# A second level of Strassen in one more product of a feed-forward, with elementwise work moved to GpSimd

## The chip, the cores and the metric

The kernel runs on one core of one Trainium2 chip. The core has five engines with a queue each: TensorE (PE; its weight loads are shown apart as PEld), VectorE (DVE), ScalarE (ACT), GpSimd (POOL) and SyncE (SP), which issues most of the DMA transfers here. TensorE writes to PSUM; the operands of all engines lie in SBUF. The metric is device time in microseconds (us) of one execution, and lower is better. A profiled execution gives, beside its time, a trace of every instruction.

## What is computed

One inference step of a decoder layer over 1040 prompt tokens and 8 sample tokens: a feed-forward, a mixer (two kinds of recurrent heads), a second feed-forward and a final norm. The change is in the two feed-forwards alone:

```
def swiglu(x, wg, wu, wd):
    return (jax.nn.silu(x @ wg) * (x @ wu)) @ wd

h = h + 0.5 * swiglu(rmsnorm(h, n1), w1g, w1u, w1d)
...
h = h + 0.5 * swiglu(rmsnorm(h, n2), w2g, w2u, w2d)
```

All in float32. The model width is 1024, the hidden width 2816.

## The kernel before

**Precision.** Each float32 operand is split into a high part, cast by ScalarE (`hi`, `cast`), and a low part, the rest, subtracted by VectorE (`lo`, `low`). A product of 128x128 weights with a block of tokens is three matmuls (`mm3`, L160): high by high, high by low, low by high.

**Tokens** are in four quarters of Q columns: 262 in the first feed-forward (1048 tokens), 258 in the second (1032). Two quarters make a half, c = 0 or 1.

**Outer level.** For one tile of 128 hidden columns, gate and up are one 2x2 block product by Winograd's form of Strassen's method: rows are gate and up, the inner dimension is the lower and upper 512 of the 1024 inputs, and columns are the two quarters of a half. There are 7 products instead of 8, numbered 1 to 7. `Left` (L443) holds a tile's four weight blocks: 1 and 2 belong to gate, 7 and 4 to up; `load` fetches one, `sum_` forms the blocks 5, 6, 7 and 3. `Blocks` holds the token side. A step of `Unit` (L493) is one product for one half c: 4 blocks of 128 inputs by 3 matmuls, 12 matmuls of Q columns. So a product of one tile has two steps. `post` adds the products up as they come: 1 to z; 6 to v; 5 to x; 7 completes up 1; 4 completes up 0; 2 is accumulated onto 1's PSUM bank and completes gate 0; 3 gives gate 1. Here 0 and 1 are the two quarters of a half. Then gate and up are multiplied by the row factor r of the norm (`times_r`), gate goes through Silu on ScalarE (`silu`), and `product_` multiplies the two to the hidden block.

**Inner level.** Tiles are taken in pairs: 11 pairs per feed-forward (`FP`). In pairs 3 to 10, product 3 of both tiles and of both halves is taken as another 2x2 product (`Inner`, L532): rows are the two tiles, columns the two halves, and the inner dimension is again split in two. Its seven products have 2 blocks by 3 matmuls each, 42 matmuls in place of 4 x 12 = 48. `begin` forms sums and differences of the two weight blocks in place, then four high and low parts; `post` (L633) adds the seven results to both tiles' temporaries. The token operands of this level are made once per feed-forward, in pair 1, by `operands` (L550).

**PSUM.** Outer results lie in pairs of banks, two such pairs at a time (`psum2`); inner ones in four single banks (`psm`).

**Hidden blocks.** `Hidden.jobs` (L936) makes, per pair, the seven token-side blocks of the down projection, again by Strassen: 1, 12, 2 and 3 are the products themselves, and 5, 6, 7 and 4 are four differences that VectorE writes to two further buffers. Seven blocks per pair are stored to DRAM (`hd`), 12 only being used for differences. `down` (L992) loads them by product and group of pairs (`Hidden.load`, L967), splits them and multiplies them with the down weights.

**Order.** In a feed-forward, PE, VectorE, ScalarE and SP execute in the order of the program text; GpSimd's order is not written out. `Steps` (L418) is a list of PE steps; `before(i, fn)` puts work of the other engines ahead of step i. A nested pair has 28 steps: 24 outer, and the inner product's seven in 4. Every work item of a pair has a step number: weights are loaded some 10 steps ahead and cast some 4 ahead of use, and hidden blocks are stored in the steps of the next pair.

**Buffers.** Weights (`r`) have 8 buffers, their split forms (`ws`) 6, temporaries (`t`) 9; of the large slots, `u` has 30 and `s` 8. An engine that is to fill a buffer waits until its last reader is done.

Of the kernel before, what the change touches and what calls it, by code (L numbers as in the profile page):

```python
# [9 lines left out]
F32 = mybir.dt.float32  # L10
# [7 lines left out]
P = 128  # L18
D = 1024
KT = D // P  # L20
NM = 16
# [421 lines left out]
class Left:  # L443
# [12 lines left out]
    def sum_(self, p):  # L456
        x, y, op = {5: (7, 4, ALU.add), 6: (5, 1, ALU.subtract), 7: (1, 7, ALU.subtract), 3: (2, 6, ALU.subtract)}[p]
        if p not in self.raw:
            self.raw[p] = self.K.raw(self.n * P)
        self.K.nc.vector.tensor_tensor(self.raw[p], self.raw[x], self.raw[y], op)  # L460
# [68 lines left out]
ORDER6 = (1, 6, 2, 5, 7, 4), (1, 2, 6, 5, 7, 4)  # L529


class Inner:  # L532
# [4 lines left out]
    def __init__(self, K, ops, op=None):  # L537
        self.K, self.ops = K, ops
        self.op = {} if op is None else op
        self.raw, self.w, self.ps = {}, {}, {}  # L540
        self.then, self.out = {}, {}

    def next(self):
        return Inner(self.K, self.ops, self.op)

    def half(self, c, h):
        n = 2 * self.K.Q
        return tuple(x[:, h * n : h * n + n] for x in self.ops[c].op[3])

    def operands(self):  # L550
# [3 lines left out]
        t = K.slot("u", K.T)  # L554
        a, b, d = t[:, :n], t[:, n : 2 * n], K.slot("s", K.T)[:, :n]
# [23 lines left out]
    def begin(self, S, s0):  # L579

        K, nc = self.K, self.K.nc
        f, g = self.raw.pop(0), self.raw.pop(1)
        tmp = K.slot("u", K.T)
        s = tmp[:, :512]
        self.z, self.v = (tmp[:, 512 + i * K.Q : 512 + i * K.Q + K.Q] for i in range(2))

        def sums():
            nc.vector.tensor_add(s[:, :256], g[:, :256], g[:, 256:])
            nc.vector.tensor_sub(s[:, 256:], s[:, :256], f[:, :256])

        def sum7():
            nc.vector.tensor_sub(g[:, :256], f[:, :256], g[:, :256])

        def sum3():
            nc.vector.tensor_sub(f[:, 256:], f[:, 256:], s[:, 256:])

        def hi(i, src):
            self.w[i] = K.ws()
            nc.scalar.copy(self.w[i][:, : src.shape[1]], src)

        def lo(i, src):
            w = src.shape[1]
            nc.vector.tensor_sub(self.w[i][:, 512 : 512 + w], src, self.w[i][:, :w].bitcast(F32))

        for at, fn, *args in (
            (2, sums), (3, sum7), (5, hi, 0, f), (6, lo, 0, f), (6, sum3), (6, hi, 1, s), (7, lo, 1, s),
            (7, hi, 2, g), (8, lo, 2, g), (9, hi, 3, f[:, 256:]), (10, lo, 3, f[:, 256:]),
        ):
            S.before(s0 + at, lambda fn=fn, args=args: fn(*args))

    def step(self, S, *ps):

        def mm():
            for p in ps:
                self.product(p)
                self.post(p)

        S.add(mm)

    def product(self, p):  # L620
# [5 lines left out]
        i, o = {1: (0, 0), 2: (0, 256), 5: (1, 0), 6: (1, 256), 7: (2, 0), 4: (2, 256), 3: (3, 0)}[p]  # L626
# [6 lines left out]
    def post(self, p):  # L633
        nc = self.K.nc
        add = nc.vector.tensor_add
        z, v, x, y = self.z, self.v, self.out[0](), self.out[1]()
# [14 lines left out]
def pair(K, S, wg, wu, f, ops, spread, hid, late_r, first=None, inner=None):  # L651
# [6 lines left out]
    fs = slice(f * P, f * P + P)  # L658
    s0 = len(S.steps)
    tm = {}  # L660
    left = Left(K, [wg[:, 0:4, fs], wu[:, 0:4, fs], wu[:, 4:8, fs], wg[:, 4:8, fs]], 4)

    def temp(n, cs):
        if n not in tm:
            tm[n] = halves(K.t(2 * K.Q))
        return tm[n][:, cs]
# [6 lines left out]
    def post(p, cs, b):  # L673
# [11 lines left out]
        elif p == 7:  # L685
            nc.vector.tensor_add(temp("u1", cs), b, temp("x", cs))
            if inner:
                times_r("u1", 1, cs)
# [6 lines left out]
        elif inner:  # L695
# [1833 lines left out]
```

## Time and profile before

| | |
|---|---|
| time, median of 3 runs | 1920.49 us (1920.16 to 1923.11) |
| the profiled execution | 1921.17 us |
| its span, first to last instruction | 1919.4 us |
| busy in it: PE, DVE, ACT, POOL | 1902.5, 1527.1, 844.2, 84.9 us |
| granted clock of TensorE, mean | 0.998 |
| matmuls | 16588 |
| DMA | 258.48 MB |

How to read it: busy time is the time in which an engine has at least one instruction under way. Matmuls are pipelined, so neighbours overlap, and the mean duration of one is longer than the distance of two. In a group of instructions stand the line, the engine, the operation, the written and the read tiles, the shapes and the count; behind the first bar, busy time in us and the mean of one in ns; behind the second, the idle time of the engine just before them and what ended it. In a timeline, the columns are start, length, engine, line, operation and tiles. In a chain of waits every piece is followed back to what released it.

### The profile page before, as it was taken

How to read it: one execution, taken by the hardware profiler on the slowest of the kernel's cores; microseconds unless marked ns; L12 is line 12 of the kernel's file. 1: busy time of each engine (PE TensorE's matmuls, PEld its weight loads, DVE VectorE, ACT ScalarE, POOL GpSimd, SP SyncE). 2: the span in 40 equal slices, each digit the busy share in tenths (PEclk: the TensorE clock that was granted, in tenths of full speed). 3: DMA queues.
4: the chain of work that ended last, by engine and by line, in shares of the span. 5: the costliest groups of instructions: out<-in, count | busy, mean ns of one | idle time of the engine just before them, and what ended most of it. 6: DMA issues, size and time to landing. Idle time of an engine off the chain costs nothing.

```text
span 1919.4 us, 41103 instructions
## 1 busy us (share of the span) xinstructions
PE 1902.5 (99%) x16588; PEld 1870.2 (97%) x16588; DVE 1527.1 (80%) x2791; ACT 844.2 (44%) x1646; POOL 84.9 (4%) x159
## 2 busy tenths in 40 slices
PE   9999999999999999999999999999999999999998
PEld 8999999999999999999999999999999999999997
DVE  7888888888788877576776667998888888878965
ACT  7632332323543644466554565742323323453353
POOL 3000000000000410000000002200000000000000
PEclk9999999999999999999999999999999999999999
DMA  8152333325977551132453154322323333597852
GB/s 241 35 151 87 103 101 96 111 90 160 299 227 254 162 164 51 50 102 69 134 139 113 54 172 149 99 85 84 111 89 102 104 95 111 163 261 232 278 180 79
DMA packets 324647, 258.48 MB, mean 135 GB/s; under 512 B 17825, under 2 KB 299681, under 8 KB 324449
## 3 DMA queue, kind: packets, MB, share of 16 engines
q1 hardware_dynamic: 324213, 255.80, 44.1%
q8 instruction: 131, 2.15, 0.5%
q14 instruction: 59, 0.48, 0.1%
q0 software_dynamic: 224, 0.04, 0.0%
q10 hardware_dynamic: 20, 0.01, 0.0%
HBM read 191.84 MB, written 64.01 MB: 133 GB/s over the span
## 4 chain that ended last, share of the span: by engine, by line
PE 91%; DVE 5%; ACT 1%; DMA 1%; issue 1%; SPq 0%; DVEq 0%; POOL 0%; POOLq 0%; ACTq 0%
PE acc L163 27%; PE acc L165 27%; PE acc L164 26%; PE mis L163 1%; PE mis L165 1%; PE mis L164 1%; PE mis L1988 1%; DMA r<-in_w_ffn_up_dram 1%; PE mis L1614 0%; PE mis L2060 0%; DVE ws L468 0%; DVE u L983 0%; PE mis L1605 0%; DVE t L303 0%; DMA u<-hd 0%
## 5 line engine op out<-in xcount | busy, mean ns | idle before, releaser
L163 PE MATMUL acc<-u,ws 128*128 128x258 f32 (+3 forms) x4210 | 1228.6, 292 | 2.2 <-ACT t L918 1.0
L165 PE MATMUL acc<-u,ws 128*128 128x258 f32 (+3 forms) x4210 | 1217.4, 289 | 0.1
L164 PE MATMUL acc<-u,ws 128*128 128x258 f32 (+3 forms) x4210 | 1216.4, 289 | 0.3 <-DVE u L306 0.2
L163 PEld LDWEIGHTS acc<-u,ws 128*128 128x128 f32 x4210 | 794.0, 189 | 9.4 <-issue 4.6
L164 PEld LDWEIGHTS acc<-u,ws 128*128 128x128 f32 x4210 | 797.5, 189 | 2.3 <-DVE u L306 0.7
L165 PEld LDWEIGHTS acc<-u,ws 128*128 128x128 f32 x4210 | 792.8, 188 | 0.6 <-DVE ws L158 0.3
L468 DVE TENSOR_TENSOR ws<-r,ws 128x512 fp32r<-128x512 f32 x268 | 184.7, 690 | 69.8 <-ACT ws L464 69.6
L464 ACT CAST ws<-r 128x512 fp32r<-128x512 f32 x268 | 155.4, 615 | 13.0 <-ACT ws L464 8.4
L460 DVE TENSOR_TENSOR r<-r,r 128x512 f32<-128x512 f32 x168 | 116.0, 692 | 1.9 <-DMA r<-in_w_ffn_up_dram 0.5
L682 ACT ACTIVATE t<-t 128x516 f32<-128x516 f32 (+1 forms) x41 | 26.2, 639 | 207.0 <-DVE t L670 207.0
L711 ACT ACTIVATE t<-t 128x516 f32<-128x516 f32 (+1 forms) x43 | 27.5, 639 | 191.7 <-DVE t L670 191.7
L983 DVE TENSOR_TENSOR u<-u,u 128x1048 fp32r<-128x1048 f32 (+3 forms) x84 | 97.0, 1157 | 5.1 <-ACT u L979 4.7
L232 POOL TENSOR_TENSOR t<-t,t 128x262 f32<-128x262 f32 (+1 forms) x56 | 54.7, 987 | 806.8 <-ACT t L231 803.6
L670 DVE TENSOR_TENSOR t<-t,u 128x516 f32<-128x516 f32 (+1 forms) x127 | 87.7, 697 | 2.8
L158 DVE TENSOR_TENSOR ws<-r,ws 128x512 fp32r<-128x512 f32 x88 | 60.9, 703 | 33.9 <-ACT ws L157 33.8
L1040 ACT CAST ws<-u 128x512 fp32r<-128x512 f32 (+1 forms) x72 | 42.1, 585 | 102.9 <-DVE u L1035 100.9
L979 ACT CAST u<-u 128x1048 fp32r<-128x1048 f32 (+3 forms) x84 | 82.8, 988 | 0.0
L1040 ACT CAST ws<-r 128x512 fp32r<-128x512 f32 (+1 forms) x84 | 47.9, 582 | 70.3 <-DVE r L1035 31.5
L1069 DVE SCALAR_TENSOR_TENSOR s<-acc,s 128x524 f32<-128x524 f32 (+3 forms) x86 | 53.7, 648 | 29.4 <-PE acc L165 29.1
L1045 DVE TENSOR_TENSOR ws<-r,ws 128x512 fp32r<-128x512 f32 (+1 forms) x84 | 57.5, 694 | 22.9 <-ACT ws L1040 22.9
L157 ACT CAST ws<-r 128x512 fp32r<-128x512 f32 x88 | 53.9, 618 | 34.9 <-PE acc L165 27.4
L1045 DVE TENSOR_TENSOR ws<-u,ws 128x512 fp32r<-128x512 f32 (+1 forms) x72 | 46.8, 650 | 26.5 <-ACT ws L1040 26.5
(465 smaller groups left out, 2341.4 us busy)
## 6 DMA issues: line engine op xcount, KB each, us to landing
r<-in_w_ffn_down_dram SPq DMA_DIRECT2D x128, 256.0 KB
hd<-s SPq DMA_DIRECT2D x93, 258.0 KB
r<-in_w_ffn_gate_dram SPq DMA_DIRECT2D x88, 256.0 KB
r<-in_w_ffn_up_dram SPq DMA_DIRECT2D x88, 256.0 KB
hd<-s SPq DMA_DIRECT2D x77, 262.0 KB
u<-hd SPq DMA_DIRECT2D x36, 516.0 KB
u<-hd SPq DMA_DIRECT2D x28, 524.0 KB
r<-in_w_in_dram SPq DMA_DIRECT2D x56, 256.0 KB
```

Of the source, the lines that this page charges most:

```text
L158: self.nc.vector.tensor_sub(lo, src, hi.bitcast(F32))
L163: mm(ps, whi, xhi, start=first, stop=False, skip_group_check=more)
L164: mm(ps, whi, xlo, start=False, stop=False, skip_group_check=more)
L165: mm(ps, wlo, xhi, start=False, stop=last, skip_group_check=more)
L460: self.K.nc.vector.tensor_tensor(self.raw[p], self.raw[x], self.raw[y], op)
L464: self.K.nc.scalar.copy(self.w[p][:, : self.n * P], self.raw[p])
L468: self.K.nc.vector.tensor_sub(t[:, 512 : 512 + w], self.raw[p], t[:, :w].bitcast(F32))
L670: nc.vector.tensor_mul(t, t if src is None else src, spread.lanes(i, cs))
L979: K.nc.scalar.copy(hi, lo.bitcast(F32))
L983: K.nc.vector.tensor_sub(lo, lo.bitcast(F32), hi.bitcast(F32))
L1040: nc.scalar.copy(w[p, j, g][:, : n * P], src)
L1045: nc.vector.tensor_sub(t[:, 512 : 512 + n * P], box[0], t[:, : n * P].bitcast(F32))
```

## The change

- Product 2 of each pair of tiles is also taken by the inner level, so pairs 3 to 10 have two inner products: N (product 2, adds to gate 0) and M (product 3, as before). The outer steps of product 2 go.
- `pair` loses its nested branch. `nested_pair` has one order of 28 PE steps for both tiles a and b (`STEPS2`), and one table of all other work by step (`PLAN2`). In the table, `d` is a load, `s` a sum, `h` and `l` a high and a low part, each with tile and product; `g` scales a gate and applies Silu; `p` is the product of gate and up; `N+` and `N-` are sums and differences of an inner product's weights; `D` is a difference of hidden blocks and `S` a store.
- Scalings of up by r, after products 7 and 4, are made by GpSimd in nested pairs; those of gate stay on VectorE.
- The four differences of hidden blocks are made by GpSimd, in all pairs, and each overwrites one of the four products: 5 overwrites 1, 7 overwrites 12, 6 overwrites 3, and 4 overwrites 2. So a difference that overwrites 1, 3 or 2 follows the store of that block.
- `sum_` of block 6 overwrites block 1 in nested pairs.
- A second set of inner token operands is made (for N), with its temporaries in `t`.
- In `down`, the first product's last group of operands is loaded and split later, and so are its first four weight pieces.

```
-    def sum_(self, p):
+    def sum_(self, p, over=None):
...
+        if over:
+            self.raw[p] = self.raw[over]
...
+    def sums(self):
+        nc, s, f, g = self.K.nc, self.s, self.f, self.g
+        nc.vector.tensor_add(s[:, :256], g[:, :256], g[:, 256:])
+        nc.vector.tensor_sub(s[:, 256:], s[:, :256], f[:, :256])
+
+    def differences(self):
+        nc, s, f, g = self.K.nc, self.s, self.f, self.g
+        nc.vector.tensor_sub(f[:, :256], f[:, :256], g[:, :256])
+        nc.vector.tensor_sub(f[:, 256:], f[:, 256:], s[:, 256:])
+
+    def src(self, i):
+        return (self.f, self.s, self.f, self.g[:, 256:])[i]
...
+STEPS2 = "a1 a6 a5 a7 b1 a4 b6 N16 N57 b5 N23 N4 b7 M16 M57 b4 M23 M4"
+
+PLAN2 = {
+    -10: "da1 da7", -9: "da4 da2", -6: "sa5 sa7", -5: "ha1", -4: "la1 sa6", -3: "ha6", -2: "la6", -1: "ha5 db1 sa3", 0: "la5 db2",
+    1: "ha7", 2: "la7 db7", 3: "hb1 db4", 4: "lb1", 6: "ha4 sb5", 7: "la4 sb7 sb6", 8: "hb6", 9: "lb6 N+ Nh0", 10: "Nl0 Nh1",
+    11: "Nl1 N-", 12: "Nh2 hb5", 13: "Nl2 lb5 Nh3", 14: "Nl3 sb3", 16: "hb7", 17: "lb7 M+ Mh0", 18: "Ml0 Mh1", 19: "Ml1 M-",
+    20: "ga0 Mh2 hb4", 21: "Ml2 lb4 gb0 Mh3", 22: "Ml3 pa0", 24: "S1", 28: "ga1", 30: "gb1 pb0", 31: "pa1", 32: "S2 D5", 33: "pb1",
+    34: "D7", 35: "S3", 36: "D6", 37: "D4", 38: "S5", 39: "S7", 42: "S6", 44: "S4",
+}
+
+def nested_pair(K, S, wg, wu, i, ops, spread, inners, hidden):
...
+    def temp(x, n):
+        n = {"g0": "z", "g1": "x", "u0": "v"}.get(n, n)
...
+    def post(x, p, b):
+        if p == 1:
+            nc.scalar.copy(temp(x, "z"), b)
+            return
+        t, y = {6: ("v", "z"), 5: ("x", "v"), 7: ("u1", "x"), 4: ("u0", "v")}[p]
+        nc.vector.tensor_add(temp(x, t), b, temp(x, y))
+        if p in (7, 4):
+            times_r(nc.gpsimd, x, t)
...
+                p, t = {"N": (2, "z"), "M": (3, "x")}[c]
+                inner.begin(lefts[0].raw[p], lefts[1].raw[p], box[0], lambda x: temp(x, t))
+                inner.sums()
...
+        if c == "g":
+            t = times_r(nc.vector, x, f"g{p}")
+            nc.scalar.activation(t, t, AF.Silu)
...
+    for at, names in PLAN2.items():
+        for name in names.split():
+            S.before(s0 + at, lambda name=name: do(name))
...
-            K.nc.vector.tensor_sub(b[p], val(x), val(y))
...
+    def block(self, hid, p):
+
+        n = {1: 0, 5: 0, 12: 1, 7: 1, 2: 2, 4: 2, 3: 3, 6: 3}[p]
+        return hid[n // 2][0][:, n % 2 * 2 * self.K.Q : n % 2 * 2 * self.K.Q + 2 * self.K.Q]
+
+    def difference(self, hid, p):
+
+        x, y = {5: (12, 1), 7: (3, 12), 6: (3, 5), 4: (2, 6)}[p]
+        self.K.nc.gpsimd.tensor_sub(self.block(hid, p), self.block(hid, x), self.block(hid, y))
...
-            at = [b + k for k in (-14, -11, -11, -9, -9, -7)], [b + k for k in (-8, -7, -6, -5, -4, -2)]
+            at = [b + k for k in (-14, -11, -11, -9, -2, -2)], [b + k for k in (-8, -7, -6, -5, 1, 2)]
...
-                    pieces(p, j, g, b + 6 * j + 2 * g, None)
+                    pieces(p, j, g, b + 6 * j + 2 * g, None, (4, 3, 2, 1)[3 * j + g] if a == 0 and 3 * j + g < 4 else 0)
...
+        inners = {"N": Inner(K, ops, 2), "M": Inner(K, ops, 3)}
...
+            if i >= 3:
+                nested_pair(K, S, wgv, wuv, i, ops, spread, inners, hidden)
+                continue
             if i == 1:
...
+                operands("M", s0 + 18, 5, s0 + 54)
+                operands("N", s0 + 40, 4, s0 + 70)
```

More of the change, by code (lines that the diff above doesn't have):

```diff
@@ L1130, in ffn, with wide @@
+        def wide():
+            n, t = 2 * K.Q, K.slot("u", K.T)
+            return t[:, :n], t[:, n : 2 * n], K.slot("s", K.T)[:, :n]
         for i in range(NF // 2):
[L1131 to L1132 removed]
+            s0 = len(S.steps)
+            if i >= 3:
+                nested_pair(K, S, wgv, wuv, i, ops, spread, inners, hidden)
+                continue
             if i == 1:
[L1135 to L1142 removed]
```

239 lines of the change are left out of this document (105 added, 134 removed).

## The prediction

> **What bounds the kernel now.** I read the page from the top: busy time, chain of work that ended last, costliest groups.
>
> ```profile
> span 1919.4 us, 41103 instructions
> PE 1902.5 (99%) x16588; PEld 1870.2 (97%) x16588; DVE 1527.1 (80%) x2791; ACT 844.2 (44%) x1646; POOL 84.9 (4%) x159
> PE 91%; DVE 5%; ACT 1%; DMA 1%; issue 1%; SPq 0%; DVEq 0%; POOL 0%; POOLq 0%; ACTq 0%
> L468 DVE TENSOR_TENSOR ws<-r,ws 128x512 fp32r<-128x512 f32 x268 | 184.7, 690 | 69.8 <-ACT ws L464 69.6
> ```
>
> TensorE is the bound over the whole span and GpSimd is nearly unused. But averages hide the stage. So next I asked for single stretches: one nested pair of feed-forward 1, and one stretch at the start of feed-forward 2 in which GpSimd works; and for VectorE's groups in the pair.
>
> ```profile
> 291.48:331.81 40.33, 40.33 (x333) 40.33 (x331) 34.95 (x61) 12.31 (x24) 0.00 (x0) 1.00 0.34 100
> 1222.00:1244.00 22.00, 22.00 (x184) 21.92 (x182) 20.75 (x29) 16.23 (x37) 13.14 (x14) 1.00 0.25 78
> ```
>
> Columns: length, then busy time of PE, PEld, DVE, ACT, POOL, then granted clock. In the pair PE is never idle and runs at full clock, 40.33 us for 330 matmuls (24 outer steps of 12, 42 inner ones): 0.1222 us each. VectorE is busy for 34.95 us, idle for 5.4.
>
> ```profile
> L468 DVE TENSOR_TENSOR ws<-r,ws 128x512 fp32r<-128x512 f32 x13 | 8.9, 688 | 4.4 <-ACT ws L464 4.4
> L697 DVE TENSOR_TENSOR t<-acc,t 128x524 f32<-128x524 f32 x2 | 1.4, 700 | 1.1 <-PE acc L165 1.1
> 299.00 0.69 DVE L468 TENSOR_TENSOR ws<-r,ws 128x512 fp32r<-128x512 f32 x1 [1.22 <-ACT ws L464]
> 326.65 0.69 DVE L954 TENSOR_TENSOR s<-s,s 128x524 f32<-128x524 f32 x1
> 327.27 0.68 DVE L460 TENSOR_TENSOR r<-r,r 128x512 f32<-128x512 f32 x1
> 327.87 0.68 DVE L468 TENSOR_TENSOR ws<-r,ws 128x512 fp32r<-128x512 f32 x1
> 307.16 0.42 DVE L603 TENSOR_TENSOR ws<-r,ws 128x256 fp32r<-128x256 f32 x1
> 307.50 0.43 DVE L641 TENSOR_TENSOR u<-mis,u 128x262 f32<-128x262 f32 x1
> ```
>
> Two readings. Of the 5.4 us idle, 4.4 are low halves that wait for ScalarE's cast, such as the 1.22 us at 299.00, and only 1.1 are waits for PE; not all of it is free. And back to back, starts lie 0.61 us apart (326.65, 327.27, 327.87) though each takes 0.69; small ones lie 0.34 apart. I count with 0.61 and 0.34.
>
> In feed-forward 2 the same instruction of two successive pairs gives the period: 1542.79 - 1503.09 = 39.70 us.
>
> ```profile
> 1503.09 0.42 DVE L588 TENSOR_TENSOR u<-r 128x256 f32<-128x256 f32 x1
> 1542.79 0.42 DVE L588 TENSOR_TENSOR u<-r 128x256 f32<-128x256 f32 x1
> ```
>
> **The change: TensorE.** In each of 8 pairs per feed-forward, 4 outer steps of product 2 (48 matmuls) become 7 inner products of 6: 42. So 324 x 0.1222 = 39.60 us, 0.73 less; in feed-forward 2, 6 x 39.70 / 330 = 0.72 less. If PE stays the bound: 8 x 0.73 + 8 x 0.72 = **11.6 us saved**.
>
> **VectorE's own work, per nested pair.** Added: low halves, three of 512 and one of 256 for two of 512, 0.61 + 0.34 = 0.95; sums and differences, four of 256, 1.36; what follows the seven inner products, seven small and one of 524, 7 x 0.34 + 0.61 = 2.99. Sum 5.3. Taken away, to GpSimd: four scalings of up and four differences, 8 x 0.61 = 4.9. The scaling of gate 0 stays, from SBUF instead of PSUM (0.61 both ways). So 34.95 + 0.4 = 35.3 us.
>
> To this come waits that stay however late VectorE is. At step 20 of the new order VectorE scales gate 0 (ga0), ScalarE then does its Silu and the cast Mh2, and VectorE's next instruction, Ml2, needs that cast: the same chain as the 1.22 us at 299.00. At steps 21 and 22, gb0 and Mh3 stand before Ml3 in the same way, with one post between: some 0.5. So 35.3 + 1.7 = **37.0 us** against PE's 39.6: 2.6 to spare.
>
> **GpSimd.** A nested pair gets 8 two-input instructions of 524 elements, where GpSimd did nothing. The trace shows this operation only at 258 and 262, and once tiny:
>
> ```profile
> L232 POOL TENSOR_TENSOR t<-t,t 128x258 f32<-128x258 f32 x28 | 23.8, 852 | 146.2 <-ACT t L231 146.1
> L1262 POOL TENSOR_TENSOR sel<-sel,s 16x8 f32<-16x8 f32 x1 | 0.2, 195 | 0.0
> 678.28 0.75 POOL L232 TENSOR_TENSOR t<-t,t 128x262 f32<-128x262 f32 x1 [1.98 <-ACT t L231]
> ```
>
> Undisturbed it takes 0.75 us at 262 and 0.195 at 8, so 0.0022 per element: some 1.3 us at 524, 8 x 1.3 = 10.5 us per pair. GpSimd has room. The question is what it does to VectorE. In the stretch from 1222:
>
> ```profile
> L354 DVE TENSOR_TENSOR u<-u,u 128x1032 fp32r<-128x1032 f32 x5 | 7.0, 1396 | 0.0
> L2128 DVE TENSOR_TENSOR s<-s,acc 128x258 f32<-128x258 f32 x13 | 5.3, 410 | 0.0
> L460 DVE TENSOR_TENSOR r<-r,r 128x512 f32<-128x512 f32 x4 | 3.7, 934 | 0.0
> L468 DVE TENSOR_TENSOR ws<-r,ws 128x512 fp32r<-128x512 f32 x4 | 3.7, 924 | 0.0
> L158 DVE TENSOR_TENSOR ws<-r,ws 128x512 fp32r<-128x512 f32 x2 | 2.1, 1038 | 0.0
> L983 DVE TENSOR_TENSOR u<-u,u 128x1032 fp32r<-128x1032 f32 x28 | 34.3, 1226 | 2.4 <-ACT u L979 2.4
> 670.66 1.25 DVE L1045 TENSOR_TENSOR ws<-r,ws 128x512 fp32r<-128x512 f32 x1
> ```
>
> Instructions with both inputs in SBUF are longer here: L460 and L468 take 934 and 924 ns instead of 690, L158 1038, L354 1396 instead of the 1226 of L983 (the same shape elsewhere). L2128, which reads PSUM, stays at 410. Lost: 5 x 0.17 + 4 x 0.24 + 4 x 0.23 + 2 x 0.35 = 3.4 us over 14 GpSimd instructions, **0.25 us each**. Where nothing reads PSUM in between, one instruction is stretched from 0.69 to 1.25 (670.66): 0.56.
>
> [...]
>
> For 524 elements the block is twice as long. The loss per instruction is 0.50 if the cover grows with it; 0.25 + 0.65 = 0.90 if the cover stays as it is; 1.1 (2 x 0.56) with no cover; nothing, if all fall into idle time or PSUM reads. By the new order's lists: after the scalings of a's up and of b's first up come SBUF instructions (lb6 and the sums; Nl2 and lb5; Ml3, pa0, sa5, sa7), so little cover; after that of b's last up come la6 and the posts of M23; differences 5 and 7 meet the posts of a6 and a5; differences 6 and 4 wait for store 3 to land and then follow in one go. I take **0.65**, nearer to the grown cover, since an outer post reads PSUM for 0.70 and not 0.41.
>
> VectorE: 37.0 + 8 x 0.65 = **42.2 us per pair**. That is over PE's 39.6 and over today's 40.33. VectorE executes in order: behind a blocked low half stand the posts that free PSUM banks, and PE waits for these. A bank is needed again some two steps after its post is due (12 x 0.1222 = 1.47 us each), so each feed-forward absorbs 2.9 us before PE stalls.
>
> **Other edits.** In pairs that aren't nested, four differences leave VectorE (2.4) and block it (4 x 0.65 = 2.6): nothing. The second set of inner operands adds 12 VectorE instructions, 7.3 us once per feed-forward, over pairs 1 to 3. Cover:
>
> ```profile
> 1371.00:1411.00 40.00, 40.00 (x336) 40.00 (x335) 32.45 (x58) 12.80 (x24) 0.00 (x0) 1.00 0.28 81
> 1803.29 7.21 DMA u<-hd
> ```
>
> Such a stretch has 7.5 us idle; I count nothing, up to 7 if that is gone. Sum 6 in place of a used block, and differences in place, save buffers; the latter make a difference wait for a store to land, on GpSimd, where only the scalings are queued behind, needed many steps later: nothing. SP issues as many transfers as before. The loads of the last operand group of down's product 1 go from 9 and 7 steps ahead of down to 2, so 6 steps, 8.8 us, before use, against 7.21 for such a load in the chain; nothing, up to 4 us twice if store 1 ahead of it is late.
>
> **Sum.** Feed-forward 1: 8 x (42.2 - 40.33) = 15.0. Feed-forward 2, in proportion: 14.7. Less 2 x 2.9: **+23.9 us**. On the profiled execution's 1921.17 that is 1945.1; on the median of the runs shown, 1920.49, it is **1944.4**. These differ by less than 0.2%, about what a measurement of this kernel can tell from no change (3.8 us).
>
> **Rivals.**
> 1. *TensorE stays the bound* (the other side). GpSimd's instructions fall into VectorE's idle time and PSUM reads. Decides: a loss below 2.6 / 8 = 0.33 each. For it: 0.25 at half the size, and VectorE waits for PE where it is ahead. Against it: the adjacent instructions above. Then -11.6: 1908.9. Up to a loss of some 0.43 it is still faster by over 0.2%. Chance 0.31.
> 2. *Break-even*: losses of 0.43 to 0.5, within 0.2%: about 1920. Chance 0.10.
> 3. *No cover*: 0.90 each, 37.0 + 7.2 = 44.2: 16 x 3.9 - 5.8 = +56, 1976; with 1.1, near 2000. [...] Chance of over 1972: 0.09.
> 4. *The differences don't come when planned*: a store's landing holds GpSimd's queue, scaled up comes late, and the products pa0 and pb0 wait. For it: difference 6 overwrites what store 3 reads. Against: pa0 stands ten steps after its scaling. At 1.5 us a pair beside a PE that is the bound: 16 x (1.5 - 0.73) = +12, 1933; inside the forecast's side. Chance 0.05.
>
> Forecast 0.45 (1928 to 1972). Faster 0.31, same 0.10, slower 0.59. The range, 1908 to 1972, takes in both signs; the forecast's own is 1928 to 1972.
>
> **What would show it.** Right: in a stretch of nested pairs VectorE near 100% busy, its 512 instructions at 0.9 us on average and PSUM reads unchanged; PE below 100%, waiting for posts (VectorE on banks); GpSimd at 1.3 us alone; pairs of 42 us. Wrong: PE at 100% and pairs of 39.6 (rival 1); GpSimd instructions long and VectorE's short, if GpSimd is the one that blocks; a gap of PE at the start of down.

## The result, and the profile after

The changed kernel takes **2000.96 us** (median of 4 runs, 1998.37 to 2003.09) against 1921.3 us of the kernel before on the same chip: ratio 1.0413, 95% interval 1.0394 to 1.0432. The forecast was 1944.4 us with a range of 1908 to 1972. The sign was right, and the time lies outside the range: +79.7 us where +23.9 stood.

The page of the kernel after, its head, the chain that ended last, and the costliest groups that answer to those of before:

```profile
span 1996.7 us, 41508 instructions
PE 1915.6 (96%) x16492; PEld 1869.0 (94%) x16492; DVE 1646.6 (82%) x2887; ACT 870.6 (44%) x1702; POOL 304.2 (15%) x311
PE 60%; DVE 27%; issue 6%; ACT 3%; DMA 3%; SPq 0%; DVEq 0%; ACTq 0%; POOL 0%; POOLq 0%
L470 DVE TENSOR_TENSOR ws<-r,ws 128x512 fp32r<-128x512 f32 x236 | 200.2, 850 | 15.4 <-ACT ws L466 13.2
L766 DVE TENSOR_TENSOR t<-acc,t 128x524 f32<-128x524 f32 (+1 forms) x128 | 88.2, 689 | 0.0
```

There are 96 matmuls fewer (16492 against 16588), and yet TensorE's share falls from 99% to 96% and its part of the chain from 91% to 60%. VectorE has 27% of the chain instead of 5%. The low halves (L470, before L468) take 850 ns each instead of 690. The posts L766, which read one of their two inputs from PSUM (so VectorE's operands don't lie in SBUF alone), take 689, as posts of this size did before (L697, 700).

How much of this arises in which stage shows at the start of `down`, that is in ScalarE's first read of its first product. The timeline of before, and that of after, in both feed-forwards:

```profile
485.68 0.60 ACT L1065 ACTIVATE s<-acc 128x524 f32<-128x524 f32 x1
1690.56 0.60 ACT L1065 ACTIVATE s<-acc 128x516 f32<-128x516 f32 x1
```

```profile
519.64 1.25 ACT L1088 ACTIVATE s<-acc 128x524 f32<-128x524 f32 x2 [1.98 <-PE acc L165]
1765.82 0.60 ACT L1088 ACTIVATE s<-acc 128x516 f32<-128x516 f32 x1 [1.94 <-PE acc L165]
```

The first delay is 519.64 - 485.68 = 34.0 us, the second 75.3, and the span has grown by 77.3. So 34.0 us arise up to the end of the nested stage of feed-forward 1, 41.3 from there to the same place in feed-forward 2, and 2.0 behind it.

One nested pair of after, between two runs of the same instruction (windows: length, then busy time of PE, PEld, DVE, ACT, POOL, granted clock):

```profile
347.03:391.18 44.15, 40.55 (x326) 39.77 (x325) 41.55 (x68) 13.60 (x27) 11.00 (x9) 1.00 0.30 91
```

And what PE waited for in the whole run, before and then after (total, times, longest). Of before, the two longest groups that lie in feed-forward code:

```profile
PE mis L163 <- DVE t L645: 1.3, 2, 0.7
PE acc L163 <- ACT t L918: 1.0, 3, 0.5
```

```profile
PE mis L163 <- DVE t L627: 21.0, 15, 2.1
PE acc L163 <- ACT t L794: 16.2, 14, 1.2
PE acc L163 <- ACT t L763: 9.6, 14, 0.8
PE acc L163 <- ACT ws L466: 7.3, 13, 0.6
```

The pair takes 44.15 us instead of 40.33; 8 x 3.82 = 30.6 of the 34.0 us are in such pairs. TensorE waits some 14 times (7 full pairs in each feed-forward) at four places, and most releasers are instructions at the end of a chain through VectorE: an inner post (L627), a Silu that waits for VectorE's scaling (L794), the copy of a product 1 queued behind it on ScalarE (L763). The fourth is a cast of weights (L466). In the pair shown the four waits are 3.6 us, of the 4.55 that it takes beyond 39.60.

How one GpSimd instruction does this shows in the timeline of after, at two places of this pair:

```profile
375.00 1.22 POOL L758 TENSOR_TENSOR t<-t,u 128x524 f32<-128x524 f32 x1 [6.54 <-DVE t L766]
375.08 1.69 DVE L470 TENSOR_TENSOR ws<-r,ws 128x512 fp32r<-128x512 f32 x1 [0.15 <-ACT ws L466]
381.97 0.69 DVE L766 TENSOR_TENSOR t<-acc,t 128x524 f32<-128x524 f32 x1
382.13 1.32 POOL L977 TENSOR_TENSOR s<-s 128x524 f32<-128x524 f32 x1 [5.90 <-DVE s L798]
382.59 1.41 DVE L470 TENSOR_TENSOR ws<-r,ws 128x512 fp32r<-128x512 f32 x1
```

At 375.00 GpSimd begins a scaling, VectorE's next instruction reads SBUF twice and lasts 1.69 us instead of 0.69: 1.00 lost. At 382.13 a post that reads PSUM is under way, so 0.53 us of GpSimd's 1.32 are covered; the low half behind it still loses 0.72.

### The profile page after: what moved, and what is told of

Read it like the earlier page. It is cut to its first block, busy times and chain, and to the rows that moved or that the text cites. A ratio compares the mean times of both kernels' runs of the same rounds, so it can differ in the third digit from the quotient of the medians.

```text
span 1996.7 us, 41508 instructions
## 1 busy us (share of the span) xinstructions
PE 1915.6 (96%) x16492; PEld 1869.0 (94%) x16492; DVE 1646.6 (82%) x2887; ACT 870.6 (44%) x1702; POOL 304.2 (15%) x311
## 4 chain that ended last, share of the span: by engine, by line
PE 60%; DVE 27%; issue 6%; ACT 3%; DMA 3%; SPq 0%; DVEq 0%; ACTq 0%; POOL 0%; POOLq 0%
PE acc L163 18%; PE acc L165 17%; PE acc L164 17%; DVE ws L470 5%; DVE r L462 5%; DVE ws L600 2%; DVE t L630 2%; DVE t L766 2%; DVE t L758 1%; ACT ws L595 1%; DVE s L798 1%; ACT ws L466 1%; DVE t L624 1%; PE mis L165 1%; PE mis L163 1%
## 5 line engine op out<-in xcount | busy, mean ns | idle before, releaser
L163 PE MATMUL acc<-u,ws 128*128 128x258 f32 (+4 forms) x3954 | 1161.7, 294 | 41.0 <-ACT t L794 16.2
L164 PE MATMUL acc<-u,ws 128*128 128x258 f32 (+4 forms) x3954 | 1147.3, 290 | 2.9 <-DVE u L1006 2.5
L165 PE MATMUL acc<-u,ws 128*128 128x258 f32 (+4 forms) x3954 | 1146.8, 290 | 0.9 <-DVE ws L470 0.4
L163 PEld LDWEIGHTS acc<-u,ws 128*128 128x128 f32 x3954 | 747.9, 189 | 56.4 <-ACT t L794 18.7
L164 PEld LDWEIGHTS acc<-u,ws 128*128 128x128 f32 x3954 | 750.8, 190 | 5.7 <-DVE u L1006 3.7
L165 PEld LDWEIGHTS acc<-u,ws 128*128 128x128 f32 x3954 | 747.3, 189 | 1.7 <-DVE ws L470 0.9
L466 ACT CAST ws<-r 128x512 fp32r<-128x512 f32 x236 | 139.4, 617 | 213.2 <-DVE r L462 207.3
L470 DVE TENSOR_TENSOR ws<-r,ws 128x512 fp32r<-128x512 f32 x236 | 200.2, 850 | 15.4 <-ACT ws L466 13.2
L758 POOL TENSOR_TENSOR t<-t,u 128x524 f32<-128x524 f32 (+1 forms) x64 | 85.1, 1330 | 406.3 <-DVE t L766 376.0
L977 POOL TENSOR_TENSOR s<-s 128x524 f32<-128x524 f32 (+1 forms) x44 | 69.0, 1569 | 259.5 <-DVE s L798 94.4
L600 DVE TENSOR_TENSOR ws<-r,ws 128x512 fp32r<-128x512 f32 (+1 forms) x96 | 83.8, 873 | 27.3 <-ACT ws L595 25.3
L163 PE MATMUL mis<-u,ws 128*128 128x258 f32 (+1 forms) x294 | 85.6, 291 | 21.0 <-DVE t L627 21.0
L794 ACT ACTIVATE t<-t 128x524 f32<-128x524 f32 (+1 forms) x64 | 40.9, 639 | 139.8 <-DVE t L758 139.8
L1063 ACT CAST ws<-u 128x512 fp32r<-128x512 f32 (+1 forms) x72 | 42.2, 586 | 107.8 <-DVE u L1058 104.4
L766 DVE TENSOR_TENSOR t<-acc,t 128x524 f32<-128x524 f32 (+1 forms) x128 | 88.2, 689 | 0.0
L165 PE MATMUL mis<-u,ws 128*128 128x258 f32 (+1 forms) x294 | 83.8, 285 | 0.0
L164 PE MATMUL mis<-u,ws 128*128 128x258 f32 (+1 forms) x294 | 83.7, 285 | 0.0
L977 POOL TENSOR_TENSOR s<-s,s 128x524 f32<-128x524 f32 (+1 forms) x44 | 65.9, 1498 | 113.5 <-DVE s L696 66.1
```

Source lines behind the costliest of these rows:

```text
L163: mm(ps, whi, xhi, start=first, stop=False, skip_group_check=more)
L164: mm(ps, whi, xlo, start=False, stop=False, skip_group_check=more)
L165: mm(ps, wlo, xhi, start=False, stop=last, skip_group_check=more)
L466: self.K.nc.scalar.copy(self.w[p][:, : self.n * P], self.raw[p])
L470: self.K.nc.vector.tensor_sub(t[:, 512 : 512 + w], self.raw[p], t[:, :w].bitcast(F32))
L600: self.K.nc.vector.tensor_sub(self.w[i][:, 512 : 512 + w], src, self.w[i][:, :w].bitcast(F32))
```

## The experiments

The theory after the result (A): GpSimd's instructions that read SBUF stop VectorE, and by this the posts come late. Rivals: (B) the order of the nested pair is late in any case, (C) work on GpSimd costs because it is somewhere else, by its waits and its queue. Each time below stands beside the kernel before on the same chip. All but the last two are single runs on several chips, on which the kernel before took 1919.83 to 1924.71 us; so two runs are compared by what each takes beyond the kernel before on its chip. For the changed kernel that is 79.7 us.

### GpSimd's instructions left out

```
-            times_r(nc.gpsimd, x, t)
+            pass
...
-        self.K.nc.gpsimd.tensor_sub(self.block(hid, p), self.block(hid, x), self.block(hid, y))
+        pass
```

The scalings of up in the nested pairs and all differences of activation blocks are left out.

> The changed kernel without its GpSimd instructions: the scalings of up in nested pairs and all differences of hidden blocks are left out (unscaled up and undiffered blocks go on). Theory A (GpSimd holds VectorE back, 0.84 us per instruction of 524, measured in the changed kernel's pair as 6.7 us over 8): VectorE's 34.9 us of its own fit under 39.6 of TensorE, pairs of 39.6 to 40.0 us, 1909 to 1920 us in all. Theory B (the new order of steps, and VectorE's waits for ScalarE's casts, stall TensorE): pairs stay at 42 us or more, over 1950. Theory C (VectorE's own added work is too much): pairs between, about 41 us, 1935 to 1950.

Measured: 1938.45 us (before 1922.11). One pair in a window:

```profile
287.52:328.20 40.68, 40.08 (x327) 39.69 (x326) 35.23 (x67) 13.62 (x26) 0.00 (x0) 1.00 0.32 100
```

The longest of PE's waits over the run:

```profile
PE mis L163 <- DVE t L627: 9.7, 16, 1.0
```

Leaving out GpSimd's instructions takes off 79.7 - 16.3 = 63 us. But the time isn't the 1909 to 1920 of theory A. It falls into the range of theory C, and not by C's cause: VectorE is busy for 35.23 us only, and the pair takes 40.68 us and not 39.6. 16.3 us over before remain; that is B of the list above. TensorE waits some 0.5 us in a pair and up to 1.0 at the end of a stage for the post of product 5 of the second inner stage, although on average VectorE has 5 us to spare. The pairs aren't all of it: they are 40.67 and, in feed-forward 2, 40.08 us long against 40.33 and 39.70 before, 6 us in 16 pairs. The other 10 us arise outside them, in part at the last pair (a wait of 1.2 for L766, one of 1.0 for L627).

### GpSimd writes only

```
-            times_r(nc.gpsimd, x, t)
+            nc.gpsimd.memset(temp(x, t), 0.0)
...
-        self.K.nc.gpsimd.tensor_sub(self.block(hid, p), self.block(hid, x), self.block(hid, y))
+        self.K.nc.gpsimd.memset(self.block(hid, p), 0.0)
```

GpSimd writes zeros where the scaled up and the differences would be.

> The changed kernel with each of these GpSimd instructions replaced by a memset of the same output tile, so that GpSimd writes SBUF but reads nothing (scaled up and the differences are zeros). [...] If writing blocks as well, or any work of GpSimd: 8 x about 0.4 us of a memset of half a microsecond, VectorE at 38 us plus 2.6 idle, some 1930 to 1950 us with stretched instructions of 1.0 us.

Measured: 1937.57 us (before 1922.11). One pair:

```profile
287.97:328.65 40.68, 40.07 (x327) 39.68 (x326) 35.27 (x68) 13.62 (x26) 4.29 (x8) 1.00 0.32 98
```

Eight instructions, of 0.54 us each, and the pair is as long as without them: 40.68, VectorE 35.27 against 35.23. By theory A, in which it is the reading that stops VectorE, nothing is held back here, and time and pair are those of the run without GpSimd: so they are (1937.57 against 1938.45), though not at the 1909 to 1920 expected of that run. The time lies in the range of the rival by which writing blocks too, but its sign, instructions of 1.0 us on VectorE, is absent; the 15.5 us over before are nearly the 16.3 of the run without GpSimd. So it is the reading that costs: with it VectorE is busy for 41.55 us in a pair (after), with writing alone for 35.27. Rival C isn't quite excluded, since these instructions are shorter than the ones they replace (0.54 us against 1.22 and more), and one of the eight starts some 6 us earlier relative to the next, as it waits for no input; but nothing in the trace speaks for it.

### The same work on VectorE, whole and by halves

All eight per pair on VectorE (`nc.vector` in both places; in the table, store 3 a step earlier, differences 6 and 4 three steps later):

> The changed kernel with all 8 back on VectorE (differences in place; store 3 one step earlier, differences 6 and 4 three steps later, so that VectorE doesn't wait for the store). Theory A: VectorE has 34.9 + 8 x 0.61 = 39.8 us of its own and 1.5 to 2.6 us of waits, pairs of 41.3 to 42.4 us, 1940 to 1962 us: faster than the changed kernel although VectorE does more, slower than before. Theory B: no faster than the changed kernel, 1995 or more. If GpSimd did relieve VectorE: 2010 or more.

Only the scalings back on VectorE, the differences on GpSimd:

> The changed kernel with the scalings of up back on VectorE; the differences stay on GpSimd. Theory A by sum (0.83 us of VectorE per GpSimd instruction against 0.61 on VectorE itself; 41.58 us a pair with none on GpSimd, 44.17 with eight): about half way, 42.5 to 43 us a pair, 1970 to 1985 us. If only the differences, three of them in a row, cost: 43.5 or more, 1990. If only the scalings, behind which posts stand, cost: 41.7, 1958.

Only the differences back on VectorE, the scalings on GpSimd. The table is that of the run with all eight, so two differences are three steps later, and not one as the expectation says:

> The changed kernel with the four differences back on VectorE (in place, one step later for two of them); the four scalings of up stay on GpSimd. If the two halves of the change on GpSimd add up, this run gives back what the other half (scalings on VectorE) left: 2001 - 1973.3 = 27.7 us for the scalings, so 1957 + 27.7 = 1985, pairs 43.2. If the cost goes by the sum of VectorE's load (each instruction moved to GpSimd saves VectorE 0.61 and costs it 0.83): all four scalings cost 4 x 0.22 = 0.9 us per pair over the kernel with all on VectorE: 42.5 and 1971.

Measured: 1957.01 us (before 1922.11), 1973.3 (1924.71) and 1971.51 (1919.83). One pair of each, in this order, each from its own trace:

```profile
293.60:335.18 41.58, 40.33 (x326) 39.72 (x325) 39.78 (x75) 13.71 (x27) 0.00 (x0) 1.00 0.32 97
```

```profile
303.19:345.41 42.22, 40.59 (x326) 39.80 (x326) 40.28 (x72) 13.61 (x26) 5.86 (x4) 1.00 0.31 95
```

```profile
296.03:338.76 42.73, 40.29 (x326) 39.69 (x325) 40.40 (x71) 13.71 (x26) 6.99 (x5) 1.00 0.31 94
```

The kernel that keeps everything on VectorE is 79.7 - 34.9 = 45 us faster than the change, as theory A had it, and still 35 us slower than before. The two halves came out as theory A by sum (1970 to 1985) and the second expectation of the last run (42.5 and 1971, by VectorE's load) had it.

Read the VectorE column: without the eight it is 35.23. Four of them on VectorE add 4 x 0.61, to 37.67. The four differences on GpSimd then cost VectorE (40.28 - 37.67) / 4 = **0.65 us** each, the four scalings (40.40 - 37.67) / 4 = **0.68**; and all eight together, in the kernel after, (41.55 - 35.23) / 8 = **0.79**. On VectorE itself each costs 0.61 by the distance of two starts, and (39.78 - 35.23) / 8 = 0.57 by the first of these windows; with 0.57 the two halves come to 0.69 and 0.72. So moving an instruction from VectorE to GpSimd takes no load off VectorE here; it adds some 0.2 us (41.55 against 39.78 for the eight).

The times of the halves don't add up: beyond the kernel with all eight on VectorE they cost 13.7 and 16.8 us, and both together 44.8. In the kernel after, the last two differences and the next pair's first scaling follow one another without a break (387.55 to 392.32), and in neither half do three; whether this makes the difference between 0.79 and 0.65 to 0.72 isn't shown.

### GpSimd's instructions in halves

Each instruction of 524 elements as two of 262.

```
-            times_r(nc.gpsimd, x, t)
+            for c in range(2):
+                s = temp(x, t)[:, c]
+                nc.gpsimd.tensor_mul(s, s, spread.lanes(int(t[1]), c))
...
-        self.K.nc.gpsimd.tensor_sub(self.block(hid, p), self.block(hid, x), self.block(hid, y))
+        n = self.K.Q
+        for c in range(2):
+            cs = slice(c * n, c * n + n)
+            self.K.nc.gpsimd.tensor_sub(self.block(hid, p)[:, cs], self.block(hid, x)[:, cs], self.block(hid, y)[:, cs])
```

> The changed kernel with each of GpSimd's instructions in nested pairs and differences made as two of half the length (262 or 258 elements). If the loss grows with the time for which a GpSimd instruction holds VectorE, less the cover of one PSUM read: 16 x 0.25 to 0.4 = 4 to 6.4 us a pair instead of 6.7, pairs of 42 to 44, 1965 to 1998 us. If each instruction costs a fixed time: worse than the changed kernel, over 2005.

Measured: 1983.71 us (before 1924.71), within the first expectation. One pair:

```profile
300.56:344.07 43.51, 40.75 (x326) 39.84 (x325) 41.05 (x67) 13.62 (x26) 14.73 (x17) 1.00 0.30 93
```

The loss falls from 0.79 to (41.05 - 35.23) / 8 = 0.73 for two halves, a small part: VectorE gains little by the break between them. Of the 21 us gained beside the changed kernel (59.0 over before instead of 79.7), the pairs, 0.64 us shorter, explain some 10.

### The kernel before, with its differences on GpSimd

```
-            K.nc.vector.tensor_sub(b[p], val(x), val(y))
+            K.nc.gpsimd.tensor_sub(b[p], val(x), val(y))
```

> The kernel before with nothing changed but the four differences per pair, made by GpSimd into the same separate buffers. Theory A counts VectorE's time: 34.95 - 4 x 0.61 + 4 x 0.84 = 35.9 us of 40.33, TensorE stays the bound, 1915 to 1927 us. A rival by which every blocked instruction delays TensorE (latency, not load) gives 44 x 0.8 us or more in sum: 1940 or more.

Measured: 1968.67 us (before 1922.11): far from theory A, and in the range of its rival. A window of about one pair (by the starts of GpSimd's instructions, pairs of 41.9 to 44.3 us occur in this kernel):

```profile
375.00:419.00 44.00, 41.93 (x330) 41.75 (x330) 35.94 (x57) 12.31 (x23) 6.35 (x4) 0.96 0.30 92
```

PE's longest wait over the run:

```profile
PE acc L163 <- DVE t L670: 27.9, 14, 2.1
```

The timeline where it arises:

```profile
375.58 5.03 POOL L954 TENSOR_TENSOR s<-s,s 128x524 f32<-128x524 f32 x3 [1.92 <-DVE s L717]
375.96 3.50 DVE L460 TENSOR_TENSOR r<-r,r 128x512 f32<-128x512 f32 x2
379.39 0.69 DVE L670 TENSOR_TENSOR t<-acc,u 128x524 f32<-128x524 f32 x1
380.22 0.36 PE L163 MATMUL acc<-u,ws 128*128 128x262 f32 x1 [2.07 <-DVE t L670]
```

VectorE is busy for 35.94 of 44.00 us, as theory A had it: by the sum of its load there is no loss. But the inputs of three differences become ready together, GpSimd does them in one go for 5.03 us, and the two sums that VectorE has at that moment take 3.50 us instead of 1.3. Behind them in VectorE's order stands L670, which scales a gate out of its PSUM bank; TensorE needs that bank and waits 2.07 us. The list has 14 such waits, in 14 of 16 nested pairs. This is the case that a sum of loads can't see.

Next, only difference 5, which comes alone, is on GpSimd:

> The kernel before with one of the four differences on GpSimd: number 5, which comes alone. The three that followed one another without a break (7, 6, 4) are back on VectorE. Theory A, the delay decides and not the sum: a single GpSimd instruction stretches one or two VectorE instructions by some 0.8 us in all, the post behind them is late by less than the two steps of slack, TensorE doesn't wait: pairs 40.3 to 40.5 (FFN1), time within 0.2% of before. Theory B, every reading GpSimd instruction costs the pair its share wherever it stands: all four cost 3.6 us per pair, one costs 0.9: pairs 41.2, some 1936.

Measured: 1923.33 us (before 1919.83). One pair:

```profile
297.33:337.66 40.33, 40.33 (x332) 40.33 (x331) 35.02 (x60) 12.31 (x23) 1.32 (x1) 1.00 0.33 100
```

The pair is 40.33 as before, and the time 0.2% longer, as theory A of this run had it. The loss on VectorE is there: 35.02 - (34.95 - 0.61) = 0.68 us. TensorE doesn't wait for it. So theory B falls, and with it the rival of the run before, that every blocked instruction delays TensorE. One instruction that comes alone is hidden here, and three in a row ahead of a post are not; whether it was the place or the number isn't shown, since a single one just ahead of L670 wasn't tried.

### The 16 us that remain without GpSimd

First, with GpSimd's work left out as in the first experiment, two sums five steps earlier than needed are put off, so that the post of product 5 isn't behind them:

```
-    -10: "da1 da7", -9: "da4 da2", -6: "sa5 sa7", -5: "ha1", -4: "la1 sa6",
+    -10: "da1 da7", -9: "da4 da2", -5: "ha1", -4: "la1 sa5 sa7 sa6",
```

> The kernel without GpSimd's instructions again (scalings of up and all differences left out), and two sums of weight blocks of the next pair (sa5, sa7) moved from in front of step 22 to behind the low half la1 at step 24. Theory B2 (what is left without GpSimd, pairs of 40.67 instead of 39.6 us, is VectorE's work bunched ahead of the post of inner product M5, for which M3 waits, 1.0 us a pair): the wait goes, pairs of 39.6 to 39.8, 1920 to 1926 us. If VectorE's sum of work sets the pair: no change, 1938.

Measured: 1932.23 us (before 1924.71), pairs still 40.55, so neither expectation held. The old wait was gone from the pair, and 0.4 us at another place had come: the copy of product 1 on ScalarE, behind a Silu that waits for VectorE. Beside the kernel before the time is 7.5 us longer instead of 16.3; the pairs, shorter by 0.13 and 0.04, explain 1.4 us of that, and where the rest was gained wasn't found.

Then a version that does all the work, with less of it on VectorE: products 6 and 5 accumulate in PSUM onto product 1, ScalarE copies the partial results out, and everything else is on VectorE, nothing new on GpSimd. The next pair's product 1 comes ahead of the last inner products, and the table of the other work is written anew (not shown).

```
+            new = p in ((1, 7) if chain else (1, 6, 5, 7))
...
+        if p in (1, 6, 5):
+            nc.scalar.copy(temp(x, {1: "z", 6: "v", 5: "x"}[p]), b)
...
+STEPS3 = "a1 m23 m4 a6 a7 a5 b1 a4 b6 N16 N57 b5 N23 N4 b7 M16 M57 b4"
```

> A version that should pass both: both inner products, nothing on GpSimd, products 6 and 5 of a tile accumulated in PSUM onto product 1, so that ScalarE's copies give v and x and four additions per pair leave VectorE (4 x 0.61); the next pair's product 1 stands ahead of M23 and M4, and weight work is spread anew, so that every post has two steps or more. By load and by latency: VectorE 37.3 of its own and few waits, TensorE the bound, pairs of 39.6 to 40.2 and 39.0 to 39.6, 1908 to 1920 us. If VectorE's load is too much after all: over 1925.

Measured: 1944.22 us (before 1924.71), pairs 40.75: over 1925, as its rival said, but VectorE is busy for only 37.95 of the 40.75. The timeline shows the one wait of a pair:

```profile
288.72 0.59 ACT L763 COPY t<-acc 128x524 f32<-128x524 f32 x1 [2.83 <-PE acc L165]
289.36 0.39 PE L163 MATMUL acc<-u,ws 128*128 128x262 f32 x1 [0.69 <-ACT t L763]
```

And the list of PE's waits its sum over the run:

```profile
PE acc L163 <- ACT t L763: 12.3, 18, 0.7
```

The copy begins as soon as the product is finished; nothing is late. The step behind it simply needs the same PSUM bank. So the steps were put in an order in which this doesn't happen (the table again follows them):

```
-STEPS3 = "a1 m23 m4 a6 a7 a5 b1 a4 b6 N16 N57 b5 N23 N4 b7 M16 M57 b4"
+STEPS3 = "a1 m23 a6 m4 a5 a7 b1 a4 b6 N16 N57 b5 N23 N4 b7 M16 M57 b4"
```

> The kernel with products 6 and 5 accumulated in PSUM and nothing on GpSimd, with another order of steps: product 4 of the second inner stage stands between products 6 and 5 of a, and a's product 7 between its product 5 and b's product 1, so that no step takes a PSUM bank that ScalarE copied only just before. Theory A, the 0.69 us per pair (about 1 with the refill) that TensorE lost there was this wait alone: pairs 39.7 to 39.9 and 39.1 to 39.4, time 1924 to 1934. Theory B, VectorE or ScalarE is late in the pair as a whole and the wait turns up elsewhere: pairs stay at 40.5 or above, 1940 or more.

Measured: 1938.28 us (before 1919.83). One pair:

```profile
287.60:327.37 39.77, 39.77 (x327) 39.60 (x326) 37.78 (x71) 15.91 (x30) 0.00 (x0) 1.00 0.34 102
```

The pairs are 39.77 us, with TensorE never idle, as theory A had it: 0.98 us less than the 40.75 of the run before, where the wait itself was 0.69. But the whole time did not follow (1924 to 1934 expected): beside the kernel before it is 18.5 us longer, after 19.5. The first and the last pair of each stage and the start of `down` have waits, and behind four of these (2.2 us at 160.10 and 2.3 at 1380.72, 1.4 at 485.10 and at 1700.65) the granted clock is 0.72 or 0.73 over the next 6 us; over the run it is 0.993. Two more runs changed the order at these ends. In the first, a's products 6 and 5 of the first pair got banks of their own again, and in the last pair the late scalings and differences stand behind the casts of `down`'s operands:

```
+TAIL_AT = [(29, 31, 34, 35, 36, 37, 38, 39, 40, 41, 42, 43, 44, 45, 47), (34, 36, 34, 35, 36, 37, 38, 39, 39, 41, 42, 42, 43, 45, 47)]
...
-            at = [b + k for k in (-14, -11, -11, -9, -2, -2)], [b + k for k in (-8, -7, -6, -5, 1, 2)]
+            at = [b + k for k in (-14, -11, -11, -9, -2, -2)], [b + k for k in (-6, -5, -4, -3, 1, 2)]
```

> The kernel with the steps set apart (pairs 39.77 and 39.13), with its two ends mended: in the first nested pair of a feed-forward, where the second inner stage has no steps yet and products 1 and 6 of a followed each other, a's products 6 and 5 get banks of their own again; in the last pair the scalings, products and differences that down needs only later come after the casts of down's operands, and those casts two steps later. Theory A, what kept that kernel above before were these ends alone: per feed-forward 3 us of waits and a half-clock stretch at the start, 5 us and another at the end; without them the pairs' gain shows, time 1912 to 1924, at or below before. Theory B, VectorE is late at the end of the nested stage by the sum of its work, and the waits move on into down: 1928 to 1938.

Measured: 1930.01 us, median of 5 runs, before 1921.63; ratio 1.0046, interval 1.0031 to 1.0061. Its timeline at the end of the second nested stage:

```profile
1682.07 1.23 DVE L1012 TENSOR_TENSOR u<-u,u 128x1032 fp32r<-128x1032 f32 x1
1683.21 0.68 DVE L1074 TENSOR_TENSOR ws<-r,ws 128x512 fp32r<-128x512 f32 x1
1683.81 0.42 DVE L627 TENSOR_TENSOR t<-mis,t 128x258 f32<-128x258 f32 x1
1684.29 0.19 PEld L163 LDWEIGHTS mis<-u,ws 128*128 128x128 f32 x1 [3.63 <-DVE t L627]
```

The time isn't that of theory A; it lies in the range of theory B, 8.4 us over before. Work for `down` that isn't due yet stands ahead of the post L627. The last run puts it behind, to see whether order or load is at fault:

```
+    plan = PLAN3 if i > 3 else PLAN3 | {8: "ha4", 9: "la4 N+", 10: "sb5 sb7 sb6 hb6 Nh0"}
...
+            at = [b + k for k in (-14, -11, -11, -9, -2, -2)], [b + k for k in (-6, -5, -2, -1, 1, 2)]
```

> The kernel with mended ends, two orders changed: at the end of the nested stage the post of the second inner stage's products 5 and 7 stands on VectorE ahead of two of down's operand low halves and of down's first weight low half (TensorE waited 3.4 us for it, and a half-clock stretch followed); in the first nested pair b's sums stand behind the post of a's product 7 (1.2 us). Theory A, order: some 1.2 us + refill at the start and 3.4 + 1.7 us at the end go, twice: 13 us less, 1915 to 1919, 0.1 to 0.4% under before. Theory B, VectorE's sum of work: the waits move on into down, 1925 to 1931.

Measured: **1921.54 us**, median of 11 runs, before 1920.71; ratio 1.0005, interval 0.9996 to 1.0014. PE's waits over the run:

```profile
PE mis L163 <- DVE t L627: 3.4, 2, 1.7
PE acc L163 <- ACT t L764: 2.6, 2, 1.4
PE acc L163 <- ACT u L1009: 1.1, 2, 0.6
```

Beside the kernel before, 7.5 us were gained (0.8 over before instead of 8.4), neither the 13 of theory A nor nothing as theory B has it. So a part at least was order. The second level of product 2, done in this way, costs as much as it saves. By this run's trace the pairs are 39.77 and 39.08 us long and save 8 x 0.56 + 8 x 0.62 = 9.4 of the 11.6 us. The waits shown, 7.1 us over both feed-forwards, lie in the first and last pairs of the nested stages. That leaves some 3 us. They seem to lie in the mixer, which the change leaves as it is: the same ScalarE instruction (L231) is 0.6 us earlier than before ahead of it (633.54 against 634.17) and 3.2 us later behind it (1185.04 against 1181.87). The cause is open. No version here beats the kernel before; one without these last waits wasn't tried.

## Why the prediction was right in its sign and wrong in its size

The mechanism that the prediction named is there: GpSimd's reads lengthen VectorE's instructions (the low halves from 690 to 850 ns on average), and the posts come late (TensorE waits up to 2.1 us for L627 and up to 2.3 for L766). The step that failed is the next one, from VectorE's work to the time: that a pair takes the longer of TensorE's 39.60 us and VectorE's sum with 1.7 us of waits, and that 2.9 us per feed-forward are absorbed. And the sign owes something to luck: without any loss this step gave 11.6 us less than before, and without GpSimd's instructions the kernel is 16.3 us slower.

- **TensorE's floor, 39.60 per pair: right**, but not where the prediction placed it. It is reached (39.77, with PE busy throughout) only in an order made for it, with the accumulation in PSUM. In the changed order it isn't reached even with GpSimd's work left out (40.68). That the rival "TensorE stays the bound" would give 1908.9 as soon as GpSimd's loss is small was wrong: without GpSimd's instructions the time is 1938.45. The 11.6 us of saving were counted as free of waits.
- **VectorE's own 35.3 us: right** (35.23). **GpSimd alone, 1.3 us at 524: right** (1.22 and 1.32).
- **Loss per GpSimd instruction, 0.65 taken: too small**; 0.79 in the changed kernel. With four on GpSimd it is 0.65 and 0.68. That the block doubles from 262 to 524 elements and that the cover grows nearly with it were the author's estimates; no run shows the 0.65 that was made of them for eight instructions. By the run in halves, one of 524 loses 0.79 and two of 262 together 0.73, so twice is about right; in the place shown, one post covers 0.53 of 1.32 us.
- **Waits that stay, 1.7 us: too small.** VectorE is idle for 44.15 - 41.55 = 2.6 us per pair. So the pair is 35.2 + 6.3 + 2.6 = 44.15 where 35.3 + 5.2 + 1.7 = 42.2 stood: of the 1.95 us, 1.1 are the loss and 0.9 the waits. (This only divides up the pair. It doesn't show that VectorE's idle time is what made it longer: in the run without GpSimd VectorE is idle for 5.4 us.) In feed-forward 2 a pair takes 43.84 us, by the timeline of after:

```profile
1594.50 1.42 DVE L581 TENSOR_TENSOR u<-r 128x256 f32<-128x256 f32 x1
1638.34 1.42 DVE L581 TENSOR_TENSOR u<-r 128x256 f32<-128x256 f32 x1
```

There 39.70 + 14.7 / 8 = 41.54 stood. Together 8 x 1.95 + 8 x 2.30 = 34 us, of the 53.4 (77.3 - 23.9) that the trace shows beyond the forecast.
- **"Each feed-forward absorbs 2.9 us": wrong.** TensorE waits in every nested pair, by PE's list of waits; and the start of `down` is 34.0 us late in feed-forward 1, more than the pairs alone (30.6). That makes 5.8 us of the 53.4, and 3.4 more. With the 34 these are 43 of the 53.4.
- **The method, VectorE's sum of work against TensorE's: the step that failed.** In the run without GpSimd's instructions the sum is 35.2 + 1.7 = 36.9 us, below 39.60, and the pair took 40.68. Applied to the kernel before with its differences on GpSimd it gave no loss (the expectation above), where 47 us were lost with VectorE idle for 8 of 44 us. In the traces the loss arises where TensorE waits for one post that stands behind lengthened instructions. Only where VectorE is nearly always busy does the sum come close: with all eight on VectorE 39.78 + 1.7 = 41.5, measured 41.58.
- **"Other edits: nothing, up to 4 us twice": wrong in its cause.** The gap of TensorE that was to be looked for at the start of `down` lies a little earlier, in the last nested pair, and there TensorE waits for VectorE and not for a load. The timeline of after:

```profile
500.95 0.36 PE L163 MATMUL acc<-u,ws 128*128 128x262 f32 x1 [2.32 <-DVE t L766]
506.90 0.41 PE L163 MATMUL mis<-u,ws 128*128 128x262 f32 x1 [2.05 <-DVE t L627]
```

And the same place in windows, where the clock falls to 0.71 and VectorE is busy for 9.87 of 10 us:

```profile
500.00:505.00 5.00, 3.90 (x30) 3.71 (x30) 4.97 (x8) 4.83 (x8) 1.32 (x1) 1.00 0.19 59
505.00:510.00 5.00, 3.10 (x15) 3.10 (x16) 4.90 (x9) 0.50 (x1) 0.17 (x1) 0.71 0.79 233
```

- **The rivals.** "No cover" gave 1976 at 0.90 and near 2000 at 1.1. The time landed there, and its pair of 44.2 at 0.90 is nearly the measured 44.15; but that is chance in part, since the loss is 0.79, and the rest is waits and what arises outside the pairs. "The differences come late" was not tried by itself; that the writes alone, most of them at the same places, cost nothing (1937.57 against 1938.45) speaks against it.
- What remains open: some 41 us were lost from the start of `down` in feed-forward 1 to that in feed-forward 2, of which the nested pairs explain 33 (8 x (43.84 - 39.70)). The other 8 lie in `down`, in the mixer and around the stage, partly in stretches of half clock (0.50 granted from 787 to 790 us and from 934 to 937 us in after), and 2 more behind it. Some 3.8 are in the mixer, by the instruction L231 of the last section (670.69 and 1222.21 against 634.17 and 1181.87); why they arise there isn't known.

## What to carry to other kernels

Price an elementwise instruction that is to go to GpSimd by what it takes from VectorE while it runs, and not by GpSimd's idle time: here 0.65 to 0.79 us against the 0.57 to 0.61 that it had cost on VectorE, so there was nothing to gain from the start. An engine that executes in order and has room on average can still be late at one place (VectorE was busy for 35.94 of 44.00 us, and TensorE waited 2.07 us for one post behind it); look up which post stands behind each instruction that gets longer, and whether several of these come together. And when matmuls are saved, write out the order at the first and the last turn of the stage too: here the turns in between gave 9.4 us of the 11.6, and waits of 7.1 us at the ends took back most of it.

## What the runs showed of the hardware that wasn't expected

A wait of TensorE cost more than its length in some places. In the kernel before with its differences on GpSimd, the matmuls behind the wait of 2.07 us that start from 380.69 to 383.74 lie 0.21 to 0.22 us apart instead of 0.12, by the timeline:

```profile
380.90 0.42 PE L164 MATMUL acc<-u,ws 128*128 128x262 f32 x1
381.12 0.42 PE L165 MATMUL acc<-u,ws 128*128 128x262 f32 x1
...
384.12 0.28 PE L164 MATMUL acc<-u,ws 128*128 128x262 f32 x1
384.24 0.29 PE L165 MATMUL acc<-u,ws 128*128 128x262 f32 x1
```

The window over it shows the granted clock, 0.83:

```profile
380.00:390.00 10.00, 9.78 (x68) 9.81 (x69) 6.38 (x10) 3.83 (x7) 0.62 (x1) 0.83 0.15 54
```

0.17 of 10 us is 1.7 us lost, nearly as much as the wait itself. Not each such wait did it, and its length alone doesn't decide. Of the 14 waits for L670 in this kernel, all of 1.85 to 2.11 us, nine have a granted clock of 0.72 over the 6 us behind them and five one of 1.00. The kernel with mended ends waits 3.44 us at the end of the first nested stage and 3.42 at the end of the second; the windows behind the two:

```profile
475.00:481.00 6.00, 6.00 (x27) 6.00 (x28) 5.95 (x11) 2.53 (x4) 0.00 (x0) 0.50 0.94 298
1684.29:1690.29 6.00, 6.00 (x50) 6.00 (x51) 5.95 (x11) 2.51 (x4) 0.00 (x0) 1.00 0.98 318
```

Two waits of the same length, and 27 matmuls in 6 us behind the one and 50 behind the other. What decides besides the length, no run here shows.
